# A hybrid decoder layer on one core: the second block's norm, its value weights and the last five products are issued in another order

## The chip, the cores and the metric

The kernel runs on one core of a Trainium2 chip. The metric is the time of one execution in device microseconds; lower is better. It was 2483.3 us before the change (median of three runs: 2478.8, 2483.3 and 2483.92). A profile is one further execution, with every instruction's start and length recorded.

## The reference, cut to what matters

One decoder layer in float32, with 2048 tokens and 1024 channels: retention and a pooling mixer side by side, cross-attention to 256 memory tokens, a gated MLP with a causal convolution, and one last norm.

```python
h = rmsnorm(x, mix_norm_g)
q, k, v, g, u = split(h @ w_in)
y_ret = silu(g) * head_rmsnorm(retention(q, k, v, positions), ret_gn_g)
y_pool = pool_mixer(u, pool_w, pool_scale)      # windows of 2, 4, 8, 16 tokens
x = x + concat(y_ret, y_pool) @ w_out
x = x + cross_attn(rmsnorm(x, xa_norm_g), mem_n, xa_wq, xa_wkv, xa_wo)
x = x + conv_glu_ffn(rmsnorm(x, ffn_norm_g), ffn_w_up, ffn_conv_w, ffn_conv_b, ffn_w_down)
out = rmsnorm(x, final_norm_g)

def rmsnorm(x, g):
    return x * rsqrt(mean(x * x, axis=-1) + EPS) * g
```

## The kernel before, in words

Channels lie on the 128 partitions and tokens along the free axis. The 2048 tokens are worked in two blocks of 1024 (`T`), each in two halves of 512 (`SUB`). Every operand of a product is held as a rounded high part and a low part that makes up the rest: ACT writes the high part and VectorE subtracts it to get the low one (`split`, L230; the lines are L233 and L216, with a gain L236 and L225). One product is then three matmuls (`passes`, L239): high by high, high by low, low by high.

A norm has these steps. VectorE adds up squares that ACT made. `stats` (L309) sums them over the partitions with narrow matmuls of one column each (L316; with a second addend also L318), and makes the factor 1/sqrt by a chain of about eleven small VectorE operations (`rsqrt`, L265). `spread` (L324) and `wide_norm` (L1242) bring the factor to all partitions: VectorE multiplies the identity by the factor's high and low parts ("diagonals"), and two matmuls with a matrix of ones (L340, L1256) copy them to every partition of a PSUM bank. ACT copies the bank to SBUF (L345, L1259).

The first part of the program runs twice, once for each block `b`. At the end of block 0 come the products of the attention's output, eight units of four quarters. A quarter is twelve matmuls on one half of the tokens (`unit`, L286); after each quarter one step of the generator in `behind[0]` is traced. While these products run, x of block 1 is loaded and squared (`load_x`, L528), and the residual's own squares are summed (`add_residual`, L806). What is left goes into `norms` (L1599), whose steps are traced after the quarters of block 1's first products, those of the pooling groups 3 and 2 (`pool_group`, L625): first the column sums of block 1's x (`nxt`), then those of block 0's own result (`xs`), needed much later, then the spread for block 1. The pooling's evacuation on VectorE needs the spread factor, `rb`. Behind the two groups the program loads and splits the four value weights (`value_weights`, L656) and makes the values from them (`values`, L667).

The weights of these products come through five raw buffers, `R`, in turn: SP loads a tile into one and it is free for the next load when its splits are done. The same SP queue carries the sums of MLP weights that are prepared beside (`weight_sums`, L906): its loads stand behind the last tile load, and POOL's accumulating transfers follow them.

The second part (`run`, L1324) is the MLP for both blocks, as rounds of seven products by which a 2 x 2 block product is made. It goes through a list of items. Each is a run of matmuls, then what is due by the clock of items (`after`, `due`), then the item's evacuation (`evac`, L1148), then up to two pending pieces such as the square, the sum of squares and the gain of a finished output tile (`out`, L1164). The last group works on members j = 2 and j = 3 of the last round, twelve matmuls an item. Its last five items are product 4 of j = 3, product 3 of j = 2 and of j = 3, and product 6 of j = 2 and of j = 3. With the first of these five, one half of block 1's tokens is complete; the other half is complete with the last. Each half then has its final norm by `ending` (L1226): column sums and factor, spread and a copy to SBUF, then eight multiplies, four or three of them on POOL, and eight stores, on the SP and ACT queues by turns.

The kernel is written with a tile framework. The order on each engine is not the order of the program: a planner, which simulates the engines' times, issues on each engine the first instruction in program order that is ready by its own clock. An edge `issue_after` holds instructions of one engine behind a given instruction of that engine, and `manual_schedule` keeps program order on the named engines.

Of the kernel before, what the change touches and what calls it, by code (L numbers as in the profile page):

```python
# [8 lines left out]
F32 = mybir.dt.float32  # L9
# [110 lines left out]
def trunk(ctx, tc, xT, memT, pos, w_qkgu, w_v, wkv, wqT, wo, wout_r, wout_p, poolT, w_up, w_dn, vecs, consts, outT):  # L120
# [118 lines left out]
    def passes(ps, lhs, rhs, start, stop, more=False):  # L239
        (lh, ll), (rh, rl) = lhs, rhs  # L240
        pe.matmul(ps, lh, rh, start=start, stop=False, skip_group_check=more)  # L241
        pe.matmul(ps, lh, rl, start=False, stop=False, skip_group_check=more)  # L242
        pe.matmul(ps, ll, rh, start=False, stop=stop, skip_group_check=more)  # L243
# [36 lines left out]
    turned = []  # L280

# [841 lines left out]
    class Down(Member):  # L1123
# [24 lines left out]
        def evac(self, i, ps):  # L1148
# [40 lines left out]
            elif self.j == KT // 2 - 1 and i == 6:  # L1189
# [3 lines left out]
                for _ in ending(self.b, 1):  # L1193
                    pass
# [3 lines left out]
        def norm(self):  # L1198
            rb = []
            if self.b == NB - 1:  # L1200
                steps = ending(self.b, 0)

                def step():
                    if next(steps, True) is None:
                        after(1, step)

                after(1, step)
# [18 lines left out]
    def ending(b, s):  # L1226

        rest = sums.pop() if s else None
        y = stats([sums[s].f[:, :SUB]], None if rest is None else rest.f[:, :SUB])
        yield  # L1230
        (ps,) = wide_norm(y, range(1), rb := [])
        yield
        for n in range(KT):
            c = 1 - s
            v = Y[n // 2].f[:, (n % 2) * T + c * SUB : (n % 2) * T + (c + 1) * SUB]
            on = pool if n in ((0, 2, 4) if s else (0, 2, 4, 6)) else dve
            tt(on, v, v, rb[0].f[:, :SUB] if on is pool else ps, ALU.mult)
            (act if n % 2 else sp).dma_start(outT[n * P : (n + 1) * P, b * T + s * SUB : b * T + (s + 1) * SUB], v)
            if n == KT // 2 - 1:
                yield  # L1240
# [69 lines left out]
    pending, later, sums, Y, fetches = [], [], [], [], []  # L1310
# [13 lines left out]
    def run(rds):  # L1324
# [49 lines left out]

        for at, (rd, g, m, i) in enumerate(items):
            clock[0] = at
            lows()
# [28 lines left out]
        while pending or waiting:  # L1406
# [3 lines left out]
            due()  # L1410
        assert not (waiting or later or pending or fetches)
# [87 lines left out]
    for b in range(NB):  # L1499
# [4 lines left out]
        rn, rb, last = normed  # L1504
        if b:
# [3 lines left out]
            wv = [value_weights(kp) for kp in range(KT // 2)]  # L1509
# [84 lines left out]
        if b + 1 < NB:  # L1594
# [4 lines left out]
            def norms(xs, nxt, normed, own):  # L1599

                normed[0] = rows_norm(nxt)
                yield
                own.append(rows_norm(xs))
                yield
                normed[1] += [TT.take() for _ in range(NS)]
                spread(normed[0], [r.f[:, :SUB] for r in normed[1]])
# [122 lines left out]
```

## Time and profile before

| what | value |
|---|---|
| median of three runs | 2483.3 us |
| profiled execution, its own time | 2477.89 us |
| its span, first to last instruction | 2476.1 us |
| TensorE busy | 2434.1 us, 98% |
| VectorE busy | 1707.3 us, 69% |
| ACT busy | 1219.5 us, 49% |
| POOL busy | 187.3 us, 8% |
| mean granted TensorE clock | 0.994 |

Times within the profile are counted from the span's start. PE is TensorE, DVE is VectorE; a releaser (`<-`) is what ended an engine's idle time before an instruction. A line such as L216 is a helper's and is shared by many operations, so that the tiles say what an operation is: `mm` and `aux` are PSUM banks, G holds x, the value weights and other split operands, Q the split weights, R raw loads, T temporaries, Z the results and residuals, `sm` the small factors. The share of busy time is an average over the whole program.

### The profile page before, as it was taken

The page shows a single profiled execution, that of the slowest core. Times are in us where ns is not written, and L with a number is a line of the kernel's source. Part 1 is how long each engine was busy: PE and PEld are TensorE (multiplying, and loading weights), DVE is VectorE, ACT ScalarE, POOL GpSimd, SP SyncE. Part 2 cuts the span into 40 slices and gives each one's busy share as a digit, 9 for nine tenths or more (in the row PEclk, how much of TensorE's full clock was granted, in tenths as well). Part 3 has the DMA queues.
Part 4 walks back from the last instruction along what each step waited for, and adds up shares of the span by engine and source line. Part 5 has one row for each costly group of instructions (what it writes and reads, how often), then busy time and mean ns, then how long its engine had stood idle before and what let it go on. Part 6 is the DMA issues. An engine that isn't in the chain of part 4 may idle for free.

```text
span 2476.1 us, 33012 instructions
## 1 busy us (share of the span) xinstructions
PE 2434.1 (98%) x11390; PEld 2034.9 (82%) x11390; DVE 1707.3 (69%) x2909; ACT 1219.5 (49%) x2171; POOL 187.3 (8%) x244
## 2 busy tenths in 40 slices
PE   6999999999999999999999999999999999999997
PEld 6888888888888888888888888888888888888885
DVE  8646576564636675574678776896767698877875
ACT  6333423443422223434655555665555577666663
POOL 1010111100121110000000100020000000000001
PEclk9999999999999999999999999999999999999998
DMA  8363889716766764366468655665446479768951
GB/s 319 93 167 115 234 198 244 230 47 200 228 140 151 157 157 151 111 216 227 156 203 278 207 182 157 230 215 168 154 160 215 135 230 307 240 189 290 333 162 68
DMA packets 257176, 474.27 MB, mean 192 GB/s; under 512 B 26864, under 2 KB 56176, under 8 KB 257008
## 3 DMA queue, kind: packets, MB, share of 16 engines
q1 hardware_dynamic: 212336, 408.18, 49.4%
q0 software_dynamic: 19584, 34.61, 9.1%
q10 hardware_dynamic: 25088, 29.37, 3.4%
q8 instruction: 89, 1.46, 0.2%
q14 instruction: 79, 0.65, 0.1%
HBM read 370.87 MB, written 170.39 MB: 219 GB/s over the span
## 4 chain that ended last, share of the span: by engine, by line
PE 94%; DVE 2%; DMA 2%; ACT 1%; issue 1%; POOL 0%; SPq 0%; POOLq 0%; ACTq 0%; DVEq 0%
PE mm L241 30%; PE mm L243 29%; PE mm L242 29%; DVE Z L216 1%; PE aux L750 1%; PE aux L851 1%; PE aux L763 1%; PE aux L243 1%; PE aux L241 1%; PE aux L242 1%; PE aux L739 1%; PE aux L765 1%; DMA VWd<-T 0%; DVE G L216 0%; DVE Q L216 0%
## 5 line engine op out<-in xcount | busy, mean ns | idle before, releaser
L241 PE MATMUL mm<-G,Q 128*128 128x512 f32 (+1 forms) x1888 | 727.6, 386 | 16.7 <-ACT Q L233 10.8
L243 PE MATMUL mm<-G,Q 128*128 128x512 f32 (+1 forms) x1888 | 725.9, 385 | 4.5 <-DVE Q L216 4.5
L242 PE MATMUL mm<-G,Q 128*128 128x512 f32 (+1 forms) x1888 | 725.2, 384 | 0.0
L242 PE MATMUL mm<-G 128*128 128x512 f32 (+1 forms) x1380 | 530.0, 384 | 0.0
L241 PE MATMUL mm<-G 128*128 128x512 f32 (+1 forms) x1380 | 528.4, 385 | 0.7 <-ACT T L491 0.7
L243 PE MATMUL mm<-G 128*128 128x512 f32 (+1 forms) x1380 | 528.3, 385 | 0.0
L241 PEld LDWEIGHTS mm<-G,Q 128*128 128x128 f32 x1888 | 358.0, 190 | 85.2 <-ACT Q L233 11.4
L243 PEld LDWEIGHTS mm<-G,Q 128*128 128x128 f32 x1888 | 357.5, 189 | 73.7 <-DVE Q L216 5.3
L242 PEld LDWEIGHTS mm<-G,Q 128*128 128x128 f32 x1888 | 358.1, 190 | 68.2 <-DVE G L216 0.4
L241 PEld LDWEIGHTS mm<-G 128*128 128x128 f32 x1380 | 259.3, 188 | 52.4 <-ACT T L491 1.2
L242 PEld LDWEIGHTS mm<-G 128*128 128x128 f32 x1380 | 259.3, 188 | 51.5
L243 PEld LDWEIGHTS mm<-G 128*128 128x128 f32 x1380 | 259.3, 188 | 51.4
L1007 ACT ACTIVATE G<-R 128x512 fp32r<-128x512 f32 (+1 forms) x272 | 167.2, 616 | 254.6 <-PE mm L242 246.5
L216 DVE TENSOR_TENSOR Q<-R,Q 128x512 fp32r<-128x512 f32 x235 | 162.6, 694 | 155.1 <-ACT Q L233 140.7
L216 DVE TENSOR_TENSOR Z<-Z,mm 128x512 f32<-128x512 f32 x284 | 193.8, 683 | 105.4 <-PE mm L243 105.0
L225 DVE SCALAR_TENSOR_TENSOR Z<-Z,vecs 128x1024 f32<-128x1024 f32 x176 | 224.7, 1280 | 50.1 <-ACT Z L1070 45.2
L216 DVE TENSOR_TENSOR G<-R,G 128x512 fp32r<-128x512 f32 (+1 forms) x268 | 178.8, 675 | 110.4 <-ACT G L1007 70.7
L233 ACT ACTIVATE Q<-R 128x512 fp32r<-128x512 f32 x150 | 93.5, 628 | 245.4 <-PE mm L242 212.7
L1007 ACT ACTIVATE Q<-R 128x512 fp32r<-128x512 f32 (+1 forms) x204 | 125.4, 615 | 96.4 <-PE mm L242 80.4
L216 DVE TENSOR_TENSOR G<-T,G 128x512 fp32r<-128x512 f32 (+1 forms) x201 | 133.0, 676 | 41.5 <-ACT G L956 28.5
L216 DVE TENSOR_TENSOR T<-T 128x512 f32<-128x512 f32 (+3 forms) x218 | 149.1, 689 | 15.6 <-ACT T L356 8.0
L1070 ACT ACTIVATE Z<-Z,vecs 128x1024 f32<-128x1024 f32 x88 | 109.1, 1241 | 34.2 <-DVE Z L216 33.3
(212 smaller groups left out, 2480.8 us busy)
## 6 DMA issues: line engine op xcount, KB each, us to landing
R<-Ud SPq DMA_DIRECT2D x176, 256.0 KB, 2.7
T<-Gd SPq DMA_DIRECT2D x168, 256.0 KB, 4.3
R<-w_up SPq DMA_DIRECT2D x132, 256.0 KB, 3.0
Gd<-Z SPq DMA_DIRECT2D x110, 256.0 KB, 2.7
Ud<-w_up SPq DMA_DIRECT2D x88, 256.0 KB, 6.2
R<-w_qkgu SPq DMA_DIRECT2D x32, 512.0 KB, 4.3
R<-Dd SPq DMA_DIRECT2D x64, 256.0 KB, 3.8
Gd<-T SPq DMA_DIRECT2D x56, 256.0 KB, 3.2
```

The lines of the kernel that those rows point to most:

```text
L216: return eng.tensor_tensor(out=out, in0=a, in1=b, op=op)
L225: dve.scalar_tensor_tensor(out=out, in0=a, scalar=s, in1=b, op0=op0, op1=op1)
L233: act.activation(hi, src, AF.Copy)
L241: pe.matmul(ps, lh, rh, start=start, stop=False, skip_group_check=more)
L242: pe.matmul(ps, lh, rl, start=False, stop=False, skip_group_check=more)
L243: pe.matmul(ps, ll, rh, start=False, stop=stop, skip_group_check=more)
L739: pe.matmul(col(sc, c), self.ch(k, c), self.ch(q, c), start=True, stop=True)
L750: pe.matmul(col(self.kv, c), col(self.kn.f, c), self.ch(v, c, h * T), start=True, stop=True)
L763: pe.matmul(col(y, c), col(self.pr.f, c), self.ch(v, c, h * T), start=True, stop=self.cur[c] is None)
L765: pe.matmul(col(y, c), self.ch(q, c), self.cur[c], start=False, stop=True)
L1007: act.activation(p2[:, 0, :w], self.raw[i].f[:, :w], AF.Copy)
L1070: act.activation(self.c[g].f, a[:, 2:], AF.Identity, bias=cb[:, f : f + 1], scale=cw[2][:, f : f + 1])
```

## The change

Four things change.

1. `norms`: its first step is empty, so that the column sums of `nxt` are traced after the second quarter and not the first. The spread is traced after the third, as before. The column sums of `xs` follow after the fifth. The TensorE instructions of each step are held behind the last matmul that was traced before them (`latest[0]`).
2. `value_weights` of block 1: its VectorE instructions are held behind the last diagonal of the spread.
3. `ending` becomes the class `Ending` with four steps, `factors`, `diagonals`, `spread` and `scaled`. For the first half the steps are traced one item apart. Its eight multiplies are all on VectorE and read PSUM, and there is no copy to SBUF: one is traced with the item before the last, four after the last item's evacuation, three between the second half's diagonals and its spread. All its stores are on the SP queue. The second half keeps three multiplies on POOL.
4. From the fifth item from the end, TensorE, VectorE and ACT issue in program order.

```diff
@@ passes
-        pe.matmul(ps, ll, rh, start=False, stop=stop, skip_group_check=more)
+        latest[0] = pe.matmul(ps, ll, rh, start=False, stop=stop, skip_group_check=more)
@@ Down.evac, after the last item
                 out(q, True)
-                for _ in ending(self.b, 1):
-                    pass
+                first = firsts[0]
+                first.scaled(range(1, 5))
+                second = Ending(self.b, 1)
+                second.factors()
+                second.diagonals()
+                first.scaled(range(5, KT))
+                second.spread()
+                second.scaled(range(KT), (0, 2, 4))
@@ Down.norm, last block
-                steps = ending(self.b, 0)
...
-                after(1, step)
+                firsts.append(Ending(self.b, 0))
+                after(1, firsts[0].factors)
+                after(2, firsts[0].diagonals)
+                after(3, firsts[0].spread)
+                after(3, lambda: pending.append(lambda: firsts[0].scaled(range(1))))
                 return
@@ 
-    def ending(b, s):
...
+    class Ending:
...
+        def factors(self):
+            rest = sums.pop() if self.s else None
+            self.y = stats([sums[self.s].f[:, :SUB]], None if rest is None else rest.f[:, :SUB])
+
+        def diagonals(self):
...
+            self.d = prs.take()
+            for i, v in enumerate((yh.bitcast(F32), yl)):
+                di = self.d.r[:, i * SUB : (i + 1) * SUB]
+                tt(dve, di.rearrange("p (a b) -> p a b", a=n), ident.rearrange("p (o b) -> p o b", o=1).to_broadcast([P, n, P]), bcast(v, P), ALU.mult)
+
+        def spread(self):
+            self.ps = aux()
+            for i in range(2):
+                pe.matmul(self.ps, ones, self.d.r[:, i * SUB : (i + 1) * SUB], start=i == 0, stop=i == 1)
+            self.d.free()
+            if self.s:
+                self.rb = TT.take()
+                act.activation(self.rb.f[:, :SUB], self.ps, AF.Copy)
+
+        def scaled(self, ns, pooled=()):
+            at = self.b * T + self.s * SUB
+            for n in ns:
+                c = (n % 2) * T + (1 - self.s) * SUB
+                v = Y[n // 2].f[:, c : c + SUB]
+                if n in pooled:
+                    tt(pool, v, v, self.rb.f[:, :SUB], ALU.mult)
+                else:
+                    tt(dve, v, v, self.ps, ALU.mult)
+                (act if self.s and n % 2 else sp).dma_start(outT[n * P : (n + 1) * P, at : at + SUB], v)
@@ run
+        ordered = ExitStack()
         for at, (rd, g, m, i) in enumerate(items):
             clock[0] = at
+            if at == len(items) - 5:
+                ordered.enter_context(tc.manual_schedule(engines={pe.engine, dve.engine, act.engine}))
...
+        ordered.close()
@@ start of block 1
-            wv = [value_weights(kp) for kp in range(KT // 2)]
+            with tc.issue_after(last.ins):
+                wv = [value_weights(kp) for kp in range(KT // 2)]
@@ norms
-                normed[0] = rows_norm(nxt)
                 yield
-                own.append(rows_norm(xs))
+                with tc.issue_after(latest[0].ins):
+                    normed[0] = rows_norm(nxt)
                 yield
                 normed[1] += [TT.take() for _ in range(NS)]
-                spread(normed[0], [r.f[:, :SUB] for r in normed[1]])
+                with tc.issue_after(latest[0].ins):
+                    normed[2] = spread(normed[0], [r.f[:, :SUB] for r in normed[1]])
+                yield
+                yield
+                with tc.issue_after(latest[0].ins):
+                    own.append(rows_norm(xs))
                 yield
```

27 lines of the change are left out of this document (10 added, 17 removed).

## The prediction

> **What bounds the kernel now.** I read the page first (busy shares, then the chain that ended last), after it the waits of TensorE, and then the timeline around each of those waits that the edit touches.
>
> ```profile
> span 2476.1 us, 33012 instructions
> ...
> PE 2434.1 (98%) x11390; PEld 2034.9 (82%) x11390; DVE 1707.3 (69%) x2909; ACT 1219.5 (49%) x2171; POOL 187.3 (8%) x244
> ...
> PE 94%; DVE 2%; DMA 2%; ACT 1%; issue 1%; POOL 0%; SPq 0%; POOLq 0%; ACTq 0%; DVEq 0%
> ```
>
> TensorE is busy for 98% of the span and makes 94% of the chain. The edit removes no product, so it can win only where TensorE idles (2476.1 - 2434.1 = 42.0 us), runs slowly, or has finished. Two such places lie in its reach. The first is the start of the second block. Its stretches (columns: length, then busy time and count of PE, PEld, DVE, ACT, POOL, then granted clock, DMA share, GB/s) and its TensorE timeline (start, length, operation, idle time before it):
>
> ```profile
> 662.24:665.65 3.41, 2.33 (x20) 2.16 (x19) 1.86 (x4) 0.86 (x2) 1.07 (x2) 1.00 0.97 326
> 665.65:669.07 3.42, 3.42 (x10) 2.68 (x9) 2.71 (x11) 1.44 (x3) 0.00 (x0) 0.51 1.05 319
> ```
>
> ```profile
> 657.57 1.84 PE L316 MATMUL aux<-consts,T 128*128 128x1 f32 x16
> ...
> 662.13 0.95 PE L316 MATMUL aux<-consts,T 128*128 128x1 f32 x8
> 664.16 1.05 PE L316 MATMUL aux<-consts,T 128*128 128x1 f32 x8 [1.08 <-DVE T L216]
> ...
> 670.76 0.47 PE L340 MATMUL aux<-G,ones 128*128 128x512 f32 x1 [0.40 <-DVE G L216]
> ...
> 684.76 0.39 PE L241 MATMUL mm<-G 128*128 128x512 f32 x1
> ```
>
> The x16 are the column sums of the next block's squares (`nxt`), the two x8 those of the block's own (`xs`). The second x8 waits 1.08 us for VectorE, and the first spread matmul (L340) 0.40 us. Right after the first wait the granted clock is 0.51 for 3.42 us, which costs 3.42 x 0.49 = 1.7 us. The last row is the first product of `values`. What VectorE did meanwhile:
>
> ```profile
> 655.54 1.29 DVE L216 TENSOR_TENSOR G<-R,G 128x512 fp32r<-128x512 f32 x2
> ...
> 661.62 0.68 DVE L216 TENSOR_TENSOR Z<-Z,mm 128x512 f32<-128x512 f32 x1
> ...
> 663.42 0.68 DVE L216 TENSOR_TENSOR T<-T 128x512 f32<-128x512 f32 x1
> ...
> 665.42 1.15 ACT L233 ACTIVATE G<-R 128x512 fp32r<-128x512 f32 x2 [2.45 <-DMA R<-w_v]
> 666.08 1.29 DVE L216 TENSOR_TENSOR G<-R,G 128x512 fp32r<-128x512 f32 x2 [1.98 <-ACT G L233]
> ...
> 667.29 0.16 DVE L222 TENSOR_SCALAR sm<-aux 128x8 f32<-128x8 f32 x1
> ...
> 669.92 1.29 DVE L216 TENSOR_TENSOR G<-consts,yh 128x512 fp32r<-128x512 f32 x2
> ```
>
> G<-R are the low parts of the value weights, which nobody reads before 684.76. They stand ahead of the residual add at 661.62 and the squares' sum at 663.42 (for which TensorE waits), and the last pair waits 1.98 us for a weight tile to land, with the whole norm (667.29 on) behind it, though its column sums were done at 657.57 + 1.84 = 659.4.
>
> The second place is the end:
>
> ```profile
> 2442.76 0.69 DVE L216 TENSOR_TENSOR Z<-Z,mm 128x512 f32<-128x512 f32 x1 [0.64 <-PE mm L243]
> 2443.48 0.63 ACT L1174 ACTIVATE T<-Z 128x512 f32<-128x512 f32 x1 [1.33 <-DVE Z L216]
> 2444.14 0.69 DVE L216 TENSOR_TENSOR T<-T 128x512 f32<-128x512 f32 x1 [0.70 <-ACT T L1174]
> 2445.48 0.69 DVE L216 TENSOR_TENSOR Z<-Z,mm 128x512 f32<-128x512 f32 x1 [0.65 <-PE mm L243]
> ...
> 2449.13 0.95 PE L316 MATMUL aux<-consts,T 128*128 128x1 f32 x8
> ...
> 2450.20 0.15 DVE L222 TENSOR_SCALAR sm<-aux 128x4 f32<-128x4 f32 x1
> ...
> 2454.16 0.39 PE L243 MATMUL mm<-G 128*128 128x512 f32 x1
> ...
> 2455.65 0.63 ACT L1174 ACTIVATE T<-Z 128x512 f32<-128x512 f32 x1 [1.68 <-DVE Z L216]
> ...
> 2457.55 2.48 DVE L216 TENSOR_TENSOR Z<-Z,aux 128x512 f32<-128x512 f32 x4 [1.33 <-ACT T L1259]
> 2457.60 4.93 POOL L216 TENSOR_TENSOR Z<-Z,T 128x512 f32<-128x512 f32 x4 [449.63 <-ACT T L1259]
> 2458.04 0.57 PE L318 MATMUL aux<-consts,T 128*128 128x1 f32 x2
> 2459.95 0.15 DVE L222 TENSOR_SCALAR sm<-aux 128x4 f32<-128x4 f32 x1
> 2460.14 1.21 DVE L222 TENSOR_SCALAR sm<-sm 128x4 int32<-128x4 int32 x1
> 2461.38 1.18 DVE L216 TENSOR_TENSOR sm<-sm 128x4 f32<-128x4 f32 x1
> ...
> 2464.17 0.17 DVE L1246 CAST yh<-sm 128x4 fp32r<-128x4 f32 x1
> ...
> 2465.06 0.68 DVE L216 TENSOR_TENSOR Q<-consts,sm 128x512 fp32r<-128x512 f32 x1
> 2465.19 1.39 PE L1256 MATMUL aux<-Q,ones 128*128 128x512 f32 x2 [6.59 <-DVE Q L216]
> 2466.62 0.60 ACT L1259 ACTIVATE T<-aux 128x512 f32<-128x512 f32 x1 [9.10 <-PE aux L1256]
> 2467.25 3.08 DVE L216 TENSOR_TENSOR Z<-Z,aux 128x512 f32<-128x512 f32 x5 [1.51 <-ACT T L1259]
> 2467.36 3.72 POOL L216 TENSOR_TENSOR Z<-Z,T 128x512 f32<-128x512 f32 x3 [4.83 <-ACT T L1259]
> ```
>
> ```profile
> GB/s 0 0 0 0 176 382 378 377 382 382 382 365 399 373 386 382 30 0 0 0 0 0 0 0 90 360 399 369 378 403 352 390 390 365 395 378 137 4 0 0
> ```
>
> After the last product (2454.16) the second half's norm is late for two reasons: it stands behind four multiplies of the first half (2457.55 to 2459.95, while its sums end at 2458.04 + 0.57 = 2458.61), and two tiny operations take 1.21 and 1.18 us instead of 0.15 to 0.17 while POOL multiplies. The GB/s row is the DMA from 2457 to 2476.1 in slices of 0.48 us: each half's 2 MB goes out at some 380 GB/s.
>
> **The change, part by part.** The sum is made against the profiled execution, 2477.89 us (its span and 1.8 us around it). The three runs are 2478.8, 2483.3 and 2483.92, so their median lies 5.4 us above it; differences are taken over to the median.
>
> *Norm a step later, column sums queued.* The two sets of sums are now two products' quarters and more apart, 16 records each, none dropped: no PE work is saved. A quarter is 12 matmuls, 2.72 us (2442.76 to 2445.48). Quarter two now runs at 657.57 to 660.29, the `nxt` sums follow to 662.13, and the own sums come after quarter five, when 663.42's sum is long there: the 1.08 us goes, and with it, I take it, the slow window after it (1.7 us). [...]
>
> *Value weights behind the spread.* Eight low parts (four times 1.29 = 5.2 us of VectorE) move behind the last diagonal; their ACT copies and SP loads are not held. The norm starts at 662.1 + 0.1, takes 2.6 us to its first diagonal (667.29 to 669.92), and two pairs of 1.29 end at 667.4; quarter three covers it (662.1 to 664.9) and quarter four most of the rest, so the 0.40 us goes too. `values` then starts at 684.76 - 3.1 = 681.7. VectorE has 14.3 us from 667.4 to there for 5.2 us of low parts and the pooling's first two halves, some seven operations of 0.6 us each or 8.4 us: 13.6 us fit even if the low parts come last, and the first quarter of `values` needs four of them. That cover is thin, and it is the main risk. Moved with them: the R buffers come free later, so on SP the next `w_qkgu` loads, and the weight sums' loads and POOL accumulations queued behind these, go later. The projections that need them start after `values`, four product pairs later; I cost that at nothing. What is late next at this place is nothing on TensorE's path. Gain 1.08 + 0.40 + 1.7 = 3.2, less 0.1 for other small stalls of a reshuffled order: 3.1 us. Bounds: 8.5 us (the rival "more") and a loss of 6.4 us (the rival "values late").
>
> *Last five products in program order.* The first half's norm runs beside products two to five. Column sums after the second (2445.28) cost the 0.95 us that they cost before at 2449.13. VectorE: chain from 2445.28 + 1.07 (2449.13 to 2450.20), 2.17 us long (2459.95 to 2464.17 less 1.21 + 1.18 and plus 2 x 0.17); then evacuation, wait for ACT's square, add, each 1.38 + 0.60 = 1.98 (2442.76 to 2444.14; 0.60 is 3.08 / 5); diagonals 1.49; twice 1.98 more. The last evacuation starts at 2445.28 + 1.07 + 2.17 + 1.98 + 1.49 + 1.98 + 1.98 = 2455.95, where it was at 2454.93 (0.72 ahead of the 2455.65): 1.0 us late. TensorE waits some 0.4 us at the spread for the diagonals, which this lateness hides.
>
> *The tail.* Square at 2456.67; sums end 2.96 later (2455.65 to 2458.61) at 2459.63; multiplies one to four fit before that. POOL has no work of the first half any more (four multiplies of 1.23 us become four of 0.60 on VectorE), so the chain takes 2.17: 2461.9. Diagonals 1.57 (2464.17 to 2465.74): 2463.5. ACT's copy 0.88 later, POOL 0.74 after that: 2465.1, ending 2468.8 in place of 2471.08: 2.25 us earlier. The stores move too: all eight of the first half are SP's, three of them (multiplies five to seven, from 2463.4) now just ahead of the second half's eight. Eleven tiles of 0.262 MB at 0.38 MB/us take 7.6 us; from 2464.1 with 0.7 us to begin and 1.7 us from the end of traffic to the span's end (the rows above: 2474.4 to 2476.1) that is 2474.1, a gain of 2.0. I take the later, 2.0. From below: if the second spread must wait for the PSUM bank that multiplies five to seven read (to 2465.3), two matmuls of 1.39 put ACT at 2466.7 and the gain is -0.1.
>
> Sum: 3.1 + 2.0 = 5.1 us. 2477.89 becomes 2472.8, and the median 2483.3 becomes 2478.2.
>
> **Rivals.**
>
> *More.* The typical run is 5.4 us slower than the profiled one. The spread hangs on a landing under a DMA share of 1.05 (ACT waits 2.45 us for it) and already holds TensorE, so each later microsecond is one lost, and another slow window may follow. If the 5.4 us sits there, the changed kernel loses it too: 2472.8. Against: the program's first loads, too, can land late.
>
> *The slow window stays or comes back elsewhere* (narrow sums still run alone, 1.84 us): 2483.3 - 1.5 - 2.0 = 2479.8. For: sums and idleness fell into one window. Against: the x16 at 657.57 alone did not slow the clock.
>
> *The end gains nothing* (the bank above): 2483.3 - 3.1 + 0.1 = 2480.3.
>
> *Values late, the other side.*
>
> ```profile
> 687.04 1.16 ACT L233 ACTIVATE Q<-R 128x512 fp32r<-128x512 f32 x2 [11.24 <-DMA R<-w_qkgu]
> 687.70 0.69 DVE L216 TENSOR_TENSOR Q<-R,Q 128x512 fp32r<-128x512 f32 x1 [8.98 <-ACT Q L233]
> ```
>
> VectorE stood still for 8.98 us there behind a late tile, unnoticed because the value weights were done at 667.37. If the planner puts low parts behind such a wait, the first two end at 688.3 + 1.3 = 689.6, 4.8 us later than 684.76, with 1.7 us of slow clock: 2483.3 + 6.5 - 2.0 = 2487.8. It decides from 686.8 on (684.76 + 2.0). Against: that tile is read only after the low parts in the program, and its buffer now comes free earlier.
>
> **How the numbers follow.** A measurement of this kernel can tell about 0.2%, 5.0 us. Chances: forecast 0.40 (2478.2, own range 2476 to 2480, 0.22 of it beyond the 5.0); more 0.28; slow window 0.08; end 0.07; values late 0.17 (0.13 of it slower by over 5.0). Faster 0.22 + 0.28 = 0.50, slower 0.13, same 0.37. The range 2472 to 2487.5 leaves out the low end of "more" and the upper half of "values late".
>
> **What would show it.** The wait of 1.08 us at L316 and 0.40 at L340 gone; no clock of 0.5 near 666 us; G<-R low parts behind the last diagonal and done before `values`, which starts near 681.7 with no wait; in the last 25 us small VectorE operations of 0.2 us, only three POOL multiplies, ACT's last copy near 2464.4 less 3.1. Wrong if TensorE waits for G<-R at `values`, if the second spread waits for multiplies five to seven, or if new waits stand between 690 and 2440.

## The result, and the profile after

The changed kernel takes 2475.18 us (median of ten runs, 2470.94 to 2478.88); the kernel before, measured beside it, 2481.27 us (ten runs, 2475.81 to 2483.92). The ratio is 0.9977, 95% interval 0.9968 to 0.9986: 6.1 us less. The profiled execution of the changed kernel took 2470.94 us, 6.95 us less than that of before; it is the fastest of its ten, so that the pair of profiles shows a little more than the medians. Line numbers shift between the kernels: L316 and L340 before are L317 and L341 after, while L1246, L1256 and L1259 of the ending before are L1244, L1254 and L1258 after.

The span and busy times on the page of the changed kernel:

```profile
span 2469.2 us, 33010 instructions
...
PE 2430.5 (98%) x11390; PEld 2032.3 (82%) x11390; DVE 1706.8 (69%) x2913; ACT 1219.9 (49%) x2170; POOL 182.9 (7%) x240
```

TensorE's busy time fell by 3.6 us with the same 11390 records, and its idle time from 42.0 to 38.7 us. To place the difference I cut both profiles at three starts: the last pair of transposes in the attention of block 0 (L851 before at 573.65, L852 after at 572.66; the later of the two starts 0.1 us further on), the first product of `values`, and the last product.

| stretch | before, us | after, us | difference |
|---|---|---|---|
| start to the last transposes of block 0 | 573.75 | 572.77 | -0.98 |
| to the first product of `values` | 111.00 | 107.46 | -3.54 |
| to the last product | 1769.40 | 1770.08 | +0.68 |
| to the end of the span | 21.95 | 18.86 | -3.09 |

The first stretch lies ahead of every edit and varies by itself (below): up to 560 us the operations of TensorE, VectorE, ACT and POOL stand in the same order in all fourteen profiles of this document. What the edits gave in this pair of profiles is 3.54 at the start of block 1 and 3.09 - 0.68 = 2.41 at the end.

**The start of block 1.** The stretches of four microseconds of the changed kernel (length, busy time and count of PE, PEld, DVE, ACT, POOL, granted clock, DMA share, GB/s), and below them TensorE's narrow sums, spread and first `values` product:

```profile
659.00:663.00 4.00, 4.00 (x28) 3.56 (x27) 1.64 (x3) 2.71 (x5) 0.00 (x0) 1.00 0.50 190
663.00:667.00 4.00, 4.00 (x19) 3.33 (x18) 3.56 (x17) 0.00 (x0) 0.00 (x0) 1.00 0.55 158
667.00:671.00 4.00, 4.00 (x23) 3.40 (x22) 4.00 (x8) 0.70 (x2) 1.60 (x2) 1.00 0.86 250
```

```profile
659.30 1.84 PE L317 MATMUL aux<-consts,T 128*128 128x1 f32 x16
...
669.45 0.48 PE L341 MATMUL aux<-G,ones 128*128 128x512 f32 x1
...
670.35 0.71 PE L341 MATMUL aux<-G,ones 128*128 128x512 f32 x2
670.90 1.17 PE L317 MATMUL aux<-consts,T 128*128 128x1 f32 x10
...
680.23 0.39 PE L241 MATMUL mm<-G 128*128 128x512 f32 x1
```

TensorE is busy for all 12 us at full clock, where before it waited 1.08 and 0.40 us and ran at 0.51 for 3.42 us. VectorE in the same place:

```profile
661.90 0.69 DVE L216 TENSOR_TENSOR Q<-R,Q 128x512 fp32r<-128x512 f32 x1 [2.36 <-ACT Q L233]
662.51 0.68 DVE L216 TENSOR_TENSOR T<-T 128x512 f32<-128x512 f32 x1
...
663.71 0.16 DVE L222 TENSOR_SCALAR sm<-aux 128x8 f32<-128x8 f32 x1
...
667.61 1.29 DVE L216 TENSOR_TENSOR G<-consts,sm 128x512 fp32r<-128x512 f32 x2
668.82 4.90 DVE L216 TENSOR_TENSOR G<-R,G 128x512 fp32r<-128x512 f32 x8
```

All eight low parts of the value weights follow the last diagonals in one run and are done at 673.7, 6.5 us ahead of `values`.

The loads changed too. These are the last value tile's load on the SP queue, first before, then after, and ACT's first copy of that tile after:

```profile
657.24 1.78 SPq L916 DMA_DIRECT2D Ud<-w_up  x3
659.11 0.54 SPq L658 DMA_DIRECT2D R<-w_v  x1
...
656.59 0.38 SPq L659 DMA_DIRECT2D R<-w_v  x1
660.20 0.63 ACT L233 ACTIVATE G<-R 128x512 fp32r<-128x512 f32 x1 [1.98 <-DMA R<-w_v]
```

Before, a load of `w_qkgu`, whose buffer a value tile's low parts have just freed, and loads of MLP weights go out ahead of it, more follow, and the tile lands 6.3 us after its issue, at a DMA share of 0.98 from 659.1 to 665.4. After, with the low parts held, the next `w_qkgu` load comes at 663.82 and the MLP weights behind it; the value tile goes out alone and lands in 3.6 us, at a share of 0.54 from 656.6 to 660.2. This holds in all fourteen profiles: 3.6 to 3.7 us in the ten with the value weights held, 6.3 to 6.9 us in the four without.

**The end.** TensorE, VectorE, ACT and POOL from the first half's spread on, which stands just ahead of the last item, and the DMA rate from 2450 to 2469.2 in slices of 0.48 us:

```profile
2447.18 0.75 PE L1254 MATMUL aux<-Q,ones 128*128 128x512 f32 x2
...
2451.28 0.68 DVE L216 TENSOR_TENSOR Z<-Z,mm 128x512 f32<-128x512 f32 x1
...
2451.99 0.63 ACT L1175 ACTIVATE T<-Z 128x512 f32<-128x512 f32 x1 [0.60 <-DVE Z L216]
...
2454.04 0.36 PE L319 MATMUL aux<-consts,T 128*128 128x1 f32 x2
2454.44 0.16 DVE L222 TENSOR_SCALAR sm<-aux 128x4 f32<-128x4 f32 x1
...
2456.60 0.17 DVE L1244 CAST yh<-sm 128x4 fp32r<-128x4 f32 x1
...
2458.09 4.87 DVE L216 TENSOR_TENSOR Z<-Z,aux 128x512 f32<-128x512 f32 x8
...
2459.80 3.72 POOL L216 TENSOR_TENSOR Z<-Z,T 128x512 f32<-128x512 f32 x3 [456.31 <-ACT T L1258]
```

```profile
GB/s 0 0 0 371 175 0 0 316 388 380 371 397 333 0 0 0 0 0 0 0 350 371 397 367 376 388 384 363 380 397 371 359 393 397 346 358 26 4 0 0
```

The second half's chain begins 0.04 us after its column sums end (2454.40), where before it began 1.34 us after them (2458.61 to 2459.95), and takes 2.16 us (2454.44 to 2456.60) where before it took 4.22 (2459.95 to 2464.17). That is 3.36 us on the path. The first half's spread now stands among the products (2447.18), where its two matmuls push the next product from 2447.18 to 2447.77; before, it ran behind the last product, where TensorE had nothing better to do. These 0.59 us make most of the +0.68 of the table. The stores take back some of the gain: POOL's last multiply ends 3.70 us earlier after the last product than before (13.22 instead of 16.92), the span 3.09. Eleven tiles leave without a break in the sixteen slices from 2459.6 to 2467.3.

### The profile page after: what moved, and what is told of

It is laid out like the page before. It is cut to its first block, busy times and chain, and to the rows that moved or that the text cites. A ratio compares the mean times of both kernels' runs of the same rounds, so it can differ in the third digit from the quotient of the medians.

```text
span 2469.2 us, 33010 instructions
## 1 busy us (share of the span) xinstructions
PE 2430.5 (98%) x11390; PEld 2032.3 (82%) x11390; DVE 1706.8 (69%) x2913; ACT 1219.9 (49%) x2170; POOL 182.9 (7%) x240
## 4 chain that ended last, share of the span: by engine, by line
PE 95%; DVE 2%; DMA 1%; ACT 1%; issue 0%; POOLq 0%; POOL 0%; SPq 0%; ACTq 0%; DVEq 0%
PE mm L241 30%; PE mm L243 30%; PE mm L242 30%; PE aux L751 1%; PE aux L852 1%; PE aux L764 1%; PE aux L740 1%; PE aux L766 1%; PE aux L243 1%; PE aux L242 1%; PE aux L241 1%; PE aux L317 1%; DVE Z L216 0%; DMA R<-wo 0%; DMA Z<-xT 0%
```

## The experiments

Where no median is given, there is one execution, the profiled one.

**The start alone.** The edits of `norms` and `value_weights` without those of `Ending` and the program order.

```diff
+            with tc.issue_after(last.ins):
+                wv = [value_weights(kp) for kp in range(KT // 2)]
...
+                with tc.issue_after(latest[0].ins):
+                    normed[0] = rows_norm(nxt)
```

> Only the start of block 1 is changed (norm a step later, column sums and value weights held); the end is that of before. If the two places are independent: from the last transpose of block 0's attention to the first product of `values` 107.5 us (before 111.0, after 107.5), no clock of 0.5 near 666 us, last product to the span's end 21.9 us as before, and about 3.5 us less in all (ratio 0.9986). Rival, the gain of the changed kernel is a chance of another order later on: the stretch from `values` to the last product moves by a microsecond or more, and the two parts do not add up.

Median 2476.45 us (11 runs) against 2480.63: ratio 0.9982, 0.9973 to 0.9991, or 4.2 us less. The stretch to `values` is 107.46 us, as in the changed kernel; the tail is 21.93 us, as before. From `values` to the last product it takes 1769.94 us, 0.54 more than before, for a wait near 1108.7 us that comes up again below.

**The end alone.** `Ending` and the program order without the edits at the start.

```diff
+                firsts.append(Ending(self.b, 0))
...
+            if at == len(items) - 5:
+                ordered.enter_context(tc.manual_schedule(engines={pe.engine, dve.engine, act.engine}))
```

> Only the end is changed; block 1 starts as before. If the places are independent: 111.0 us from the last transpose to `values` with the wait of 1.08 us and the clock of 0.5 near 666 us, `values` to last product 1770.1 us (0.7 more than before, for the spread that now stands among the products), last product to end 18.9 us, about 2.4 us less in all (ratio 0.999). Rival, the stores limit the end: the tail stays above 20 us.

Median 2478.45 us: ratio 0.9990, 0.9981 to 0.9999, or 2.2 us less. Tail 18.87, from `values` to the last product 1770.04: a gain of 3.08 less 0.64, as in the changed kernel. The two parts add up within their intervals: 4.2 + 2.2 = 6.4 beside 6.1. The slow clock of the end began earlier in this profile, 3.63 us after the last product and not 5.32, and the chain began 0.3 us later for it (4.44 us after the last product and not 4.14), yet the tail is the same as in the changed kernel: with the stores going out without a break, these 0.3 us of the chain no longer reach the end. This kernel has the start of before, and its stalls there are others than those of the profile of before: no wait for the column sums and no slow window, but one wait of 2.38 us in TensorE's timeline, and 110.35 us to `values`:

```profile
671.33 0.47 PE L341 MATMUL aux<-G,ones 128*128 128x512 f32 x1 [2.38 <-DVE G L216]
```

**The kernel before, profiled again.** No edit.

> The kernel before, unchanged, for a second profile. Theory (the waits at the start of block 1 are there in every execution but vary with the landing of the value weights' tiles; the slow window needs a window of 3.4 us that holds few wide matmuls, and so depends on how the windows fall): the stretch from the last transposes to `values` is 109.3 (no slow window) to 111.5 us, and the tail 21.95, within 0.1. Rival (1.08 and 0.40 us of waiting and the slow window always come together, as the prediction had it): 111.0 us, within 0.2, with the clock at 0.5 near 666 us.

The stretch to `values` is 112.99 us, beyond the range that I had given, and the tail 21.98. TensorE, VectorE and ACT of this execution:

```profile
660.71 1.05 PE L316 MATMUL aux<-consts,T 128*128 128x1 f32 x8 [1.31 <-DVE T L216]
...
673.63 0.47 PE L340 MATMUL aux<-G,ones 128*128 128x512 f32 x1 [2.19 <-DVE G L216]
```

```profile
668.98 1.29 DVE L216 TENSOR_TENSOR G<-R,G 128x512 fp32r<-128x512 f32 x2 [2.31 <-ACT G L233]
```

```profile
668.31 1.15 ACT L233 ACTIVATE G<-R 128x512 fp32r<-128x512 f32 x2 [2.78 <-DMA R<-w_v]
```

The last value tile lands 6.6 us after its issue, ACT waits 2.78 us for it, VectorE 2.31 us behind ACT, and the norm and TensorE (2.19 us) behind VectorE. So the start of before costs 2.89 (the end alone), 3.54 (before) and 5.53 us (before again) more than 107.46. Six of the seven profiles that have the changed start without redundant column sums (the changed kernel, the start alone, and four of the five below) have 107.44 to 107.46; the seventh, the kernel without program order, has 108.37. The gain at this place is the removal of a stall that varies by execution, and its mean over the three is 4.0 us.

**The steps of the norm alone.** `norms` as after, the value weights not held.

```diff
-                normed[0] = rows_norm(nxt)
                 yield
+                with tc.issue_after(latest[0].ins):
+                    normed[0] = rows_norm(nxt)
```

> The norm's steps are those of the changed kernel, but the value weights are free to go first. Theory: what TensorE waited for was the late sum of the block's own squares; with those column sums after quarter five the 1.08 us and the slow window (1.7 us) go, while VectorE is still held by the last value tile's landing, so that the spread may wait longer than 0.40 us: 108 to 109 us from the last transpose to `values`. Rival, the value weights ahead of the norm are the whole cause: 110 us or more.

Median 2481.62 us, ratio 1.0001, 0.9992 to 1.0010. The stretch to `values` is 109.82 us, between the range of the theory and that of the rival. TensorE waits for no engine between 640 and 700 us, and yet the clock falls, as three stretches of 3.41 us show:

```profile
667.83:671.24 3.41, 3.41 (x18) 2.84 (x17) 3.04 (x14) 0.00 (x0) 0.56 (x1) 1.00 1.07 319
671.24:674.65 3.41, 3.30 (x21) 2.68 (x20) 2.02 (x4) 0.60 (x1) 1.50 (x3) 1.00 1.04 398
674.65:678.06 3.41, 3.41 (x10) 2.63 (x9) 0.00 (x0) 0.00 (x0) 0.45 (x2) 0.50 1.09 308
```

The second stretch holds the own column sums between the spread matmuls, and TensorE is busy for 3.30 of 3.41 us. A wait of TensorE is not what the third stretch's 0.50 follows.

**The value weights alone,** held behind the spread, with the norm's steps as before; run twice.

```diff
-            wv = [value_weights(kp) for kp in range(KT // 2)]
+            with tc.issue_after(last.ins):
+                wv = [value_weights(kp) for kp in range(KT // 2)]
```

> The value weights are held behind the spread, and the norm's steps are those of before. Theory: VectorE then has the own squares' sum ready near 660 us, ahead of the column sums at 662, so the 1.08 us and the slow window go without the later step: 107.5 to 108 us from the last transpose to `values`. Rival, the step's place is needed: a wait of about 1 us at the column sums and a clock of 0.5 behind it, 110 us or more.

> The value weights' low parts behind the spread, all else as before, for a second profile and more times. Theory (what this edit alone gains sits between the last transposes of block 0 and the first product of `values`: 107.5 us where before has 111.0; what the earlier times showed against it was the head's own spread of some 8 us): the same stretch is again 107.5 us, within 0.2, and the median lies 2 to 4 us under before. Rival (the gain is paid back somewhere in block 1 or the profile was a lucky one): the stretch is 109 us or more, or the stretch is 107.5 and the median within 1.5 us of before.

The stretch to `values` is 107.54 us in both profiles, with no wait of TensorE in it: this edit alone takes the whole stall away. But the medians are 2481.34 us (ratio 0.9999, 0.9989 to 1.0009) and 2479.51 us (0.9999, 0.9989 to 1.0008): the kernel is not faster, as the rival of the second expectation had it. Both profiles are late before they reach the edit, 579.57 and 577.92 us to the last transposes, where the other twelve profiles have 572.77 to 576.78. What differs there is waits and slow windows of the first 550 us, for instance 3.4 us at half clock from 279.2 us on in the one, and 6.8 us of it from 55.9 us on in the other. The mean granted clock of the two sets of ten runs is 0.9939 and 0.9938, that of the eleven runs of the start alone 0.9950; 0.0011 of 2480 us is 2.7 us, an estimate of what slow windows cost this kernel more. The order of the operations up to 560 us is the same. Why this kernel should meet more slow windows, with an edit that lies behind those seen, I could not settle, and that this edit alone gains time is therefore shown for its stretch and not for the whole.

**Column sums three times.** The changed kernel, with the sums of `nxt` done three times; the two further passes are redundant.

```diff
-        for t, ap in enumerate(cols):
+        for t, ap in [c for c in enumerate(cols) for _ in range(times)]:
...
-                    normed[0] = rows_norm(nxt)
+                    normed[0] = rows_norm(nxt, 3)
```

> The changed kernel with the column sums of the next block's squares done three times over (redundant work, 32 records more, about 3.6 us of narrow matmuls at one stretch, TensorE never idle). Theory (the clock falls after a window of about 3.4 us in which wide matmuls fill less than about 0.4, idle or not): a granted clock of 0.5 for about 3.4 us just after these sums, and the stretch from the last transposes to `values` grows from 107.5 by 3.6 + 1.7 = 5.3 us. Rival (idle time of TensorE makes the clock fall): the clock stays at 1.0 there and the stretch grows by 3.6 us alone.

The sums in the trace, and the stretches around them, cut where the clock changed:

```profile
660.62 8.03 PE L317 MATMUL aux<-consts,T 128*128 128x1 f32 x48
```

```profile
659.60:663.01 3.41, 3.41 (x29) 3.21 (x27) 2.09 (x4) 1.86 (x4) 0.00 (x0) 1.00 0.48 153
663.01:666.42 3.41, 3.41 (x19) 3.41 (x18) 1.21 (x2) 2.71 (x5) 0.00 (x0) 0.50 0.42 159
666.42:669.84 3.42, 3.42 (x14) 3.23 (x15) 1.68 (x8) 0.00 (x0) 0.00 (x0) 0.50 0.44 137
669.84:673.25 3.41, 3.41 (x9) 2.64 (x8) 3.14 (x13) 0.00 (x0) 0.81 (x1) 0.50 0.84 291
```

The stretch to `values` grew to 115.90 us. TensorE is never idle, and the clock is 0.50 for three windows. So the clock fell here with no idle time of TensorE: in the window before the fall it was busy for 3.41 of 3.41 us. The size was off: the slow clock began within the sums, so that the 32 records more took 6.2 us and not 3.6, and three windows were slow and not one.

**Low parts twice.** The changed kernel, with each low part of the value weights computed twice.

```diff
+            for _ in range(times - 1):
+                tt(dve, u.r[:, i * T + SUB : (i + 1) * T], r, u.f[:, i * T : i * T + SUB], ALU.subtract)
...
-                wv = [value_weights(kp) for kp in range(KT // 2)]
+                wv = [value_weights(kp, times=2) for kp in range(KT // 2)]
```

> The changed kernel with each of the eight low parts of the second block's value weights computed twice (redundant work, 8 x 0.61 = 4.9 us more of VectorE; TensorE's order is the same). Theory (the low parts were done at 673.7, 6.5 us ahead of `values` at 680.23, so the cover is thick enough for 4.9 us more): TensorE does not wait for them, and the stretch from the last transposes to `values` stays at 107.5 us, within 0.3. Rival (the prediction's count: 13.6 us of VectorE work in 14.3 us): `values` starts 3.5 to 4.5 us later, with a wait on VectorE in front of it, and perhaps 1.7 us of slow clock behind it.

107.46 us to `values`, with no wait. VectorE's first fourteen low parts, and TensorE's first product of `values`:

```profile
670.96 4.90 DVE L216 TENSOR_TENSOR G<-R,G 128x512 fp32r<-128x512 f32 x8
676.37 3.70 DVE L216 TENSOR_TENSOR G<-R,G 128x512 fp32r<-128x512 f32 x6
...
682.39 0.39 PE L241 MATMUL mm<-G 128*128 128x512 f32 x1
```

Fourteen of the sixteen are done by 680.1, the last two run at 680.59 and 681.86, with other work of VectorE between and behind them. The cover bears 4.9 us more.

**No program order.** The changed kernel, with the last five products left to the planner.

```diff
-            if at == len(items) - 5:
-                ordered.enter_context(tc.manual_schedule(engines={pe.engine, dve.engine, act.engine}))
```

> The changed kernel with the last five products left to the planner's order instead of the program's. Theory (half of the end's gain is VectorE being done with the first half's multiplies before the second half's column sums are, which the program order sets): the second chain starts 2 us or more behind its column sums' end, and the tail is 20.5 to 22 us instead of 18.9. Rival (taking POOL out of the way does it all): tail 18.9, within 0.3.

The tail is 21.82 us, and all but 0.1 us of the end's gain is gone. (The 1769.97 us from `values` to the last product hold no spread here, but 0.6 us of the wait near 1108 us. The start was 108.37 us; the part on the value weights below says why.) The second half's last column sums, VectorE's multiplies of the first half, and the first operation of the chain:

```profile
2454.50 4.87 DVE L216 TENSOR_TENSOR Z<-Z,aux 128x512 f32<-128x512 f32 x8 [0.59 <-PE aux L1254]
...
2455.55 0.36 PE L319 MATMUL aux<-consts,T 128*128 128x1 f32 x2
2459.29 0.15 DVE L222 TENSOR_SCALAR sm<-aux 128x4 f32<-128x4 f32 x1
```

All eight multiplies are ahead of the chain, which begins 3.38 us after its sums (2455.91). It is short (2.16 us) with POOL at rest, but what that gives is lost to the four multiplies that came over from POOL.

**Four on POOL.** The changed kernel, with multiplies one to four of the first half on POOL again, the order kept.

```diff
-                first.scaled(range(1, 5))
+                first.scaled(range(1, 5), range(1, 5))
...
-            if self.s:
+            if True:
```

> The changed kernel with multiplies one to four of the first half given back to POOL (the spread copied for them by ScalarE), the program order kept. Theory (POOL's multiplies make VectorE's tiny operations slow): the second half's chain takes 4.2 us instead of 2.16, with two or more operations of about 1.2 us, and the time from the last product to the end grows from 18.9 to about 20.5 to 21 us. Rival (the order alone made the gain): the chain stays at 2.2 us and the tail at 18.9, within 0.3.

The tail is 19.16 us, 0.3 more than in the changed kernel, and the stretch before it 0.2 more, which a wait near 1110 us explains (0.3). The chain took 2.17 us and not 4.2, as the rival had it, but the run could not tell the two apart: POOL's four multiplies end at 2458.90, and the chain begins at 2458.94, as their timeline shows.

```profile
2454.22 4.68 POOL L216 TENSOR_TENSOR Z<-Z,consts 128x512 f32<-128x512 f32 x4 [446.49 <-DVE Z L216]
...
2458.94 0.16 DVE L222 TENSOR_SCALAR sm<-aux 128x4 f32<-128x4 f32 x1 [2.48 <-PE aux L319]
```

**POOL under the chain.** As the next kernel, but with multiplies one to six on POOL.

```diff
-                first.scaled(range(1, 5))
+                first.scaled(range(1, 7), range(1, 7))
...
-                first.scaled(range(5, KT))
+                first.scaled(range(7, KT))
...
```

> As the kernel with two multiplies on POOL, but with multiplies one to six of the first half there, so that POOL (six times 1.24 us from about 2450.0) is at work until about 2457.4, over the whole of the second half's chain, while VectorE has only its own chain to do. Theory (POOL's multiplies make VectorE's tiny operations wait): two or more operations of the chain take 1.0 to 1.3 us instead of 0.16, and the chain from the first of them to the diagonals is 4 to 5 us instead of 2.45. Rival (the 1.21 and 1.18 us before came from something else, VectorE's own multiplies or the slow clock): all of the tiny operations stay at 0.15 to 0.17 us.

The timeline of POOL and VectorE:

```profile
2451.91 6.78 POOL L216 TENSOR_TENSOR Z<-Z,consts 128x512 f32<-128x512 f32 x6 [446.54 <-DVE Z L216]
...
2456.63 0.16 DVE L222 TENSOR_SCALAR sm<-aux 128x4 f32<-128x4 f32 x1 [2.48 <-PE aux L319]
2456.82 0.84 DVE L222 TENSOR_SCALAR sm<-sm 128x4 int32<-128x4 int32 x1
2457.70 1.00 DVE L216 TENSOR_TENSOR sm<-sm 128x4 f32<-128x4 f32 x1
2458.74 0.36 DVE L225 SCALAR_TENSOR_TENSOR sm<-sm,sm 128x4 f32<-128x4 f32 x2
```

POOL's multiplies take 6.78 / 6 = 1.13 us each in the mean; taken singly, the fifth ends at 2457.64 and the sixth at 2458.69. The two slow operations end 0.01 to 0.02 us after these (2456.82 + 0.84 and 2457.70 + 1.00): each ends as the POOL instruction under way does. The first operation of the chain, which reads PSUM, is not slowed (0.16 us), nor is any after POOL's end (0.36 us for the two from 2458.74 on). From the first operation to the diagonals it is 3.97 us instead of 2.45, and the tail 20.15 us. That the 1.21 and 1.18 us before came by POOL's multiplies is shown: those two ended 0.03 and 0.02 us after its third and fourth (2461.32 and 2462.54). The size is a little under what I expected, since POOL ran out after two operations. The two that were slow are a `tensor_scalar` and a `tensor_tensor` on SBUF; what in POOL's work holds them up no run shows.

**Two on POOL, in an attempt at a faster kernel.** ScalarE's copy of the first half's spread is made early, multiplies five and six of the first half go to POOL, seven stays.

```diff
+                first.scaled((5, 6), (5, 6))
                 first.scaled(range(1, 5))
...
-                first.scaled(range(5, KT))
+                first.scaled(range(7, KT))
...
+                after(3, lambda: pending.append(lambda: (firsts[0].copied(), firsts[0].scaled(range(1)))))
```

> The changed kernel with ScalarE's copy of the first half's spread made early and multiplies five and six of the first half given to POOL before the second half's norm begins; seven stays on VectorE. Theory (the changed kernel's end is set by eleven tiles that leave at 380 GB/s from the eighth multiply on, and by POOL being free while VectorE works; POOL would be done at about 2452.5, two us before the chain begins): nine tiles are left, the tail is 17.4 to 17.9 us instead of 18.86, the median 1 to 1.4 us under the changed kernel's and 6.5 to 7.5 us under before. Rival (POOL beside VectorE slows the last squares' sums): the chain starts 0.3 to 1 us later and the tail is 18.3 to 19.2 us.

Median 2474.61 us (11 runs) against 2480.84: ratio 0.9977, 0.9968 to 0.9986, the same as that of the changed kernel. The tail of the profile is 19.41 us, longer than the rival said. POOL, VectorE and TensorE at the end:

```profile
2454.38 2.59 POOL L216 TENSOR_TENSOR Z<-Z,consts 128x512 f32<-128x512 f32 x2 [446.49 <-DVE Z L216]
...
2455.07 0.95 DVE L216 TENSOR_TENSOR T<-T 128x512 f32<-128x512 f32 x1
...
2456.17 0.35 PE L317 MATMUL aux<-consts,T 128*128 128x1 f32 x2 [1.07 <-DVE T L216]
...
2459.23 0.56 PE L319 MATMUL aux<-consts,T 128*128 128x1 f32 x2
2459.83 0.16 DVE L222 TENSOR_SCALAR sm<-aux 128x4 f32<-128x4 f32 x1 [0.82 <-PE aux L319]
```

POOL was done 2.27 us after the last product, about where I had it, but it slowed a sum of squares (0.95 us instead of 0.69), and the last column sums fell into the slow clock (0.56 us a pair instead of 0.36; from the first pair to the end of the last 3.62 us instead of 2.89). The chain begins 5.13 us after the last product, not 4.14: 0.26 us by POOL, 0.73 by the clock. From its first operation on, the end is 14.28 us instead of 14.72. That does not price the two stores: the end alone, with all eleven and a chain that began 0.3 us later than in the changed kernel, has 18.87 - 4.44 = 14.43 us there.

## Why the prediction was right or wrong

The prediction was 2478.2 us from 2483.3, 5.1 us less, with a range of 2472 to 2487.5. The result is 2475.18 from 2481.27, 6.1 us less: inside the range, just below the likeliest case's own 2476 to 2480, and of the sign that had most of the chance. Both places gave somewhat more than their terms. That the slow window was in the profile that the sum was made against, and that the start's gain came out near its term, is luck in part, as follows.

*Norm a step later.* Right: the waits of 1.08 and 0.40 us are gone, and the sums of `nxt` end at 661.14 (662.12 with the 0.98 of the first stretch added back; predicted 662.13). Wrong in the working: "the norm starts at 662.1 + 0.1". It starts at 663.71, some 2.5 us later than that, because two low parts of split weights (Q<-R), the first of which waits 2.36 us for ACT, stand ahead of it on VectorE. The diagonals end at 668.90 and not, as the prediction had it, by 667.4 less the 0.98. It cost nothing, since TensorE had products enough.

*The slow window.* The step "and with it, I take it, the slow window after it (1.7 us)" had the right gain for this profile by the wrong cause. What the clock followed shows in a count. In the profile of before the clock changes at 47.88, 665.70, 669.11 and 2457.69 us, that is, after 181, 1 and 524 times 3.4133 us. Counting the starts of 128x512 matmuls in the windows of 3.41 us of such a grid, from 640 to 700 us, where a dense window has 15: the clock fell after a window with 3 (before), 1 (before again), 4 (sums three times) and 6 (norm steps alone), and in none of the fourteen profiles after one with 7 or more; five profiles had windows of exactly 7. In these windows idle time, narrow sums or a stretched spread took the place of wide matmuls, and where the windows begin differs by execution: from the span's start, the changes lie 0.10 us past a multiple of 3.4133 us in the profile of before, and 1.44 us past one in that of the changed kernel. The count is one of this stretch alone: elsewhere in the profile of before the clock stayed at 1.00 after a window of 6 such starts and 20 matmuls of 128x128 (from 293.64 us on) and after one of 2 and 26 (from 341.43 us on). The changed kernel's poorest window had 9; the start alone, with the same start, had two of 7, one more than the 6 after which the clock fell in the norm steps alone. So the 1.7 us is a term with a chance: two of three profiles with the start of before had it, and the one without it had the longest single wait, 2.38 us. An estimate of the chance: a grid of windows of 3.41 us, laid over the recorded starts at every position, has a window of six or fewer at 97, 100 and 84% of the positions in these three profiles, and at none in the changed kernel. No idle time is needed for it: with the sums three times the clock fell after a window in which TensorE was busy for 3.41 of 3.41 us, and after the wait of 2.38 us in the end alone it did not fall.

*Value weights behind the spread.* The gain was mis-sized, 3.1 against 3.54 in this pair and 4.0 as the mean over three profiles of the old start: the sum took one execution's waits for the waits of the kernel. Right: the cause (the norm behind a late value tile). Incomplete: how the edit helps. The prediction had the norm wait for its column sums alone after the change; it still waits for the last value tile, through ACT, whose copies of that tile come ahead of the Q<-R copy that VectorE needs first. In seven of the eight profiles with both edits of the start the first diagonal ends 6.9 us after ACT begins to copy the tile (after: 660.20 to 667.10; the eighth has the column sums three times). What helps is also that the tile lands in 3.6 us instead of 6.3, since the later loads, which the prediction moved back and costed "at nothing", no longer share the DMA with it. The margin is small: counted from the last transposes, ACT's copy began at 86.3 to 88.9 us in the six profiles without a loss, and at 89.99 in the kernel without program order, where the spread follows the diagonals and `values` is the 0.9 us late. Wrong: "that cover is thin, and it is the main risk". The low parts were done 6.5 us ahead of `values`, and 4.9 us more of them changed nothing. The count of 8.4 us of other VectorE work failed: some 5.5 us of it (673.64 to 679.18) stand ahead of `values`, behind the low parts and not in front of them.

*Last five products and the tail.* The lateness of the last evacuation was 0.9 us (0.68, and 2451.28 - 2450.30 against 2454.93 - 2454.16 makes 0.21 more); predicted 1.0. Its cause was partly another: I had TensorE wait 0.4 us at the spread, and it does not wait, but the spread's own two matmuls, which I gave no cost, delay the products by 0.59 us, most of the 0.68. Then the step "sums end 2.96 later" was mis-sized: they end 2.41 us after the square (2451.99 to 2454.40), since before they had run in the slow clock (0.57 us a pair, now 0.36). Where the slow clock begins behind the last product differs by execution (2.99 to 5.74 us over the fourteen profiles), so that these 0.5 us are luck. The chain was as predicted (2.17; 2.16), and so was the time of the eleven stores, 7.6 us by the prediction and 7.7 in the trace. The end gave 2.4 us and not 2.0. One point was understated: the prediction gave half of the tail's gain to POOL's absence, but without the program order that alone gives nothing.

*Rivals.* "Values late" did not come. "The end gains nothing" was refuted: the second spread at 2457.72 runs while the multiplies of the first half read their bank. "The slow window stays or comes back", whose 1.5 us are the waits of 1.08 and 0.40, did not come, but came in the norm steps alone. "More" was half right: the start of before does vary, by 2.6 us over three profiles, and once cost 5.5 us. But the spread of 8 us among the ten runs is as wide in the changed kernel as before (in the start alone and with two multiplies on POOL eleven runs lie within 3.6 us), and the first stretch, which no edit touches, varies from 572.77 to 579.57 us over the fourteen profiles.

*New waits.* In the profile of the changed kernel none stands between 690 and 2440 us: the two of 0.9 and 0.3 us there are those of before. But the sign that the prediction named did come elsewhere. In six of the eight profiles with both edits of the start TensorE waits 0.14 to 0.75 us near 1110 us for VectorE (L852 behind L220), and what follows is 0.3 to 0.95 us late; in the six other profiles it waits at most 0.06 us there. ACT works ahead of VectorE at this place and waits itself for a stored intermediate to land (T<-Hd; 5.09 us in the start alone, 4.34 before). The counts speak for the edits of the start as the cause; no run shows how.

## What to carry to other kernels

One profile of a stall that hangs on a DMA landing is one draw: look for what loosens the dependence (here, low parts that nobody needs yet standing ahead of a norm that TensorE needs, and loads that nobody needs yet beside the one that it hangs on), follow it through every engine, and price it over several executions (it cost 2.89, 3.54 and 5.53 us here). Keep matmuls of one column apart from waits and from each other, since the clock here followed what the wide matmuls filled of a window (it fell after 1 to 6 starts of 128x512 in 3.41 us, and not after 7 or more, between 640 and 700 us), not whether TensorE was busy (3.41 of 3.41 us ahead of one fall). At the end of a program look at the order on VectorE first: whatever stands between the last column sums and their chain is paid until the stores become the limit (3.38 us without the program order), and small VectorE operations with SBUF inputs should not run beside POOL's multiplies (0.84 to 1.21 us here instead of 0.16).

## What was not expected of the hardware

The granted clock fell to 0.50 with TensorE busy for 3.41 of 3.41 us (the sums three times), in windows of mostly 128x1 matmuls (4 wide starts in the first, 0 in the second). VectorE's operations of 0.16 us took 0.84 to 1.21 us beside POOL, ending with the POOL instruction under way, while one that reads PSUM kept its 0.16 us. A tile of 512 KB landed in 3.6 to 3.7 us when its load went out alone and in 6.3 to 6.9 us beside other loads.
